# One FFN stage of a Trainium2 encoder block, fed with the un-normalized activations in 512-column matmuls, with the normalization applied to its results

## The chip, the cores and the metric

The kernel runs on one core of one Trainium2 chip. The metric is device time in microseconds (us), the median of several executions; before the change it is 2491.45 us (three runs, 2491.24 to 2491.88). The core has a matrix engine (TensorE, PE in the profile), three engines for elementwise work (VectorE, DVE in the profile; ScalarE, ACT; GpSimd, POOL) and a queue engine (SyncE, SP) that issues most loads. Each takes its own list of instructions, and they wait for one another through semaphores. The numbers of lines (L175 and so on) are those of the kernel before, unless it is said that they belong to the changed kernel.

## What is computed

One encoder layer over 512 tokens of 2048 features, in float32. The change lies in the last third, the SwiGLU feed-forward part:

```python
        u = rms_norm(h, ffn_pre_g[l])
        gate, up = jnp.split(u @ w_gate_up[l], 2, axis=-1)
        f = (jax.nn.silu(gate) * up) @ w_down[l]
        h = h + rms_norm(f, ffn_post_g[l])
```

`rms_norm(h, g)` is h times g (by feature) divided by the root of the mean square of h (by token). D_FF is 5632, so `gate` and `up` have 44 blocks of 128 features each; block j of both together is called pair j here. Activations are kept transposed: 16 tiles of 128 features by 512 tokens.

## The kernel before

**Precision.** A float32 matrix product is made of three matmuls on a rounded format (fp32r): an operand is split into a rounded copy ("hi", a cast on ScalarE) and a remainder ("lo", source minus copy, a subtraction on VectorE), and hi x lo, hi x hi and lo x hi are added up in PSUM. Weights come in chunks of 128 x 1024 (`wchunk`: one load on the SP queue into one of five `raw` buffers, one cast `whi`, one remainder `wlo`; `whi` and `wlo` have three buffers each). Activations are split in 512 columns (`split`), or 256 token columns at a time into one tile whose left half is the copy and whose right half the remainder (`merged`, L166 to L171).

**The feed-forward stages.** The residual stream h2 lies in the 16 tiles `f[i]`. Its split copies `u[i]`, scaled by ffn_pre_g but not by the 1/rms per token, are made on the way (`h2`, L886). Pairs 0, 1 (`interleaved`, tiles f0_0 to f0_3 in PSUM) and pair 2 (`gemm`, f0_4 and f0_5) are multiplied from `u` in 512 columns. The 1/rms, which becomes known after the last h2 tile, is made by `rstd` (four small matmuls r_s, a scale, a power on GpSimd) and spread over the partitions by `by_column` (matmuls r_b, then a copy on ScalarE into the tile `r3`, L922). For these three pairs r3 is applied to the results (L927, L928), since it commutes with the product. silu is on ScalarE (L929), the product of both halves on GpSimd (L930), and the store `a_d` on ScalarE's queue (L931).

**The stage f1** computes pairs 4 and 5 of the title, which the code numbers 3 and 4, counted from zero. It loops over eight weight chunks c (from `w_g0[1]`, rows 2c and 2c + 1 of the reduction). For each i = 2c + k it multiplies `f[i]` by ffn_pre_g and r3 in place (L943), splits it with `merged` into two half-token blocks (b1 for i under 8, b2 from 8 on), and multiplies these in 256 columns (`plain`, L175 to L177: 384 matmuls in all). For i from 8 on it also makes the differences of the Winograd form of Strassen's scheme (`winograd_t`, L219 to L222: four subtractions) and splits them (t12, t34). b11, b2, t12 and t34 are the operands of all later pairs, 5 to 43 (`strassen`, L287 to L336), each of which takes 7 products of quarters.

**What sets the order.** The kernel is recorded in program order, and a scheduler then orders each engine's list by priorities and by its estimate of times, and hands out buffers; an instruction marked with `keep_in_program_order` stays in its place among the marked ones of its engine. In this stage of the kernel before almost nothing is marked. On the chip each list runs in order.

Of the kernel before, what the change touches and what calls it, by code (L numbers as in the profile page):

```python
# [74 lines left out]
def hybrid_block(ctx: ExitStack, tc, xT, vecs, rpb, mask, w_c0, w_qk, w_v, w_gg, w_cg, w_ao, w_co, w_out, w_g0, w_gu, w_dn, outT):  # L75
# [60 lines left out]
    def wchunk(src, name, parts=1, cast=nc.scalar.copy, raw=None, load=nc.sync.dma_start):  # L136
# [5 lines left out]
        for n in range(parts):  # L142
            s = slice(n * w // parts, (n + 1) * w // parts)
            if not loaded:
                load(raw[:, s], src[:, s])
            cast(hi[:, s], raw[:, s])  # L146
            nc.vector.tensor_tensor(out=lo[:, s], in0=raw[:, s], in1=hi[:, s].bitcast(F32), op=ALU.subtract)  # L147
# [18 lines left out]
    def merged(src, name):  # L166

        t = slot(name, F32R)
        nc.scalar.copy(t[:, A], src)  # L169
        nc.vector.tensor_tensor(out=t[:, B], in0=src, in1=t[:, A].bitcast(F32), op=ALU.subtract)  # L170
# [2 lines left out]
    def plain(o, hi, lo, t, first, last):

        nc.tensor.matmul(o, hi, t[:, B], start=first, stop=False, skip_group_check=True)  # L175
        nc.tensor.matmul(o, hi, t[:, A], start=False, stop=False, skip_group_check=True)  # L176
        nc.tensor.matmul(o, lo, t[:, A], start=False, stop=last, skip_group_check=True)  # L177

    def gemm(outs, acts, name, n=None, more=None, cols=slice(0, NT), between=(), pin=False, raw=None, load=nc.sync.dma_start):
# [36 lines left out]

    def winograd_t(u1, u2, t12, t34):

        nc.vector.tensor_tensor(out=t12[:, A], in0=u1[:, B], in1=u1[:, A], op=ALU.subtract)  # L219
# [700 lines left out]
    gemm(  # L920
        [(pf[4 + n], w_gu[n * FT + 2]) for n in range(2)], u, "f0",
        between=(lambda: nc.scalar.copy(r3, by_column(r, "r3", pin=True)),),  # L922
    )
    for j in range(3):
        t = stp.tile([P, 2, NT], F32, tag="S", name=f"sg{j}")
        t, up = t[:, 0], t[:, 1]
        nc.vector.tensor_tensor(out=t, in0=pf[2 * j], in1=r3, op=ALU.mult)  # L927
        nc.vector.tensor_tensor(out=up, in0=pf[2 * j + 1], in1=r3, op=ALU.mult)  # L928
        nc.scalar.activation(t, t, AF.Silu)  # L929
        nc.gpsimd.tensor_tensor(out=t, in0=t, in1=up, op=ALU.mult)  # L930
        nc.scalar.dma_start(a_d[j], t)  # L931
# [3 lines left out]
    b11, b2, b_t12, b_t34 = [], [], [], []  # L935
    pf = [bank(f"f1_{n}") for n in range(4)]
    for c in range(HT):
        hi, lo = wchunk(w_g0[1, c], f"f1_{c}")
        if c == HT - 1:
            first = begun(w_gu[5], "f5")  # L940
        for k in range(2):
            i = 2 * c + k
            nc.vector.scalar_tensor_tensor(out=f[i], in0=f[i], scalar=col(C_FPRE, i), in1=r3, op0=ALU.mult, op1=ALU.mult)  # L943
# [414 lines left out]
```

## Time and profile before

| what | us |
|---|---|
| median of three runs | 2491.45 |
| span of the profiled execution (first to last instruction) | 2489.2 |
| the median less that span: start and end, which the span leaves out | 2.25 |
| PE busy in the span | 2464.8 (99%) |
| DVE busy | 2073.3 (83%) |
| ACT busy | 1246.1 (50%) |
| POOL busy | 493.3 (20%) |
| stage f1 on PE, first matmul to the first of pair 5 | 1211.02 to 1257.09 |

The page gives no time of its own for the profiled execution other than the span. A busy share says that an engine had an instruction in flight; matmuls overlap, so the time that one costs is read from the distance of two starts, not from its duration. A bracket at a row's end tells how long the engine had been idle and what ended the wait.

### The profile page before, as it was taken

Reading aid. Unit: us, or ns where it says so; the run is one execution under the profiler, and the core shown is the slowest. Engines: PE = TensorE matmul, PEld = TensorE weight load, DVE = VectorE, ACT = ScalarE, POOL = GpSimd, SP = SyncE. Lnnn points to the kernel's source line nnn. Section 1 sums busy time; section 2 is a strip of 40 time slices with the busy share of each in tenths; the row PEclk is TensorE's granted clock in tenths of the full one; section 3 lists DMA queues with packets and bytes.
Section 4 is the critical chain, followed back from the end, with each engine's and each line's share of the span. In section 5 each row is a group of like instructions: output and inputs, shape, how many; then the busy total and the mean of one; then the engine's idle time right before and its main releaser. Section 6 shows DMA issues by size and latency. Waiting matters only on the chain. (4 is left out here: it accounts for less than half of the span.)

```text
span 2489.2 us, 36170 instructions
## 1 busy us (share of the span) xinstructions
PE 2464.8 (99%) x13495; PEld 2141.7 (86%) x13495; DVE 2073.3 (83%) x2743; ACT 1246.1 (50%) x1939; POOL 493.3 (20%) x583
## 2 busy tenths in 40 slices
PE   9999999999999999999999999999999999999997
PEld 8888888888888888889998888888888888888887
DVE  5999887497777668878898888889898889989887
ACT  5223333355555434556455555555555565456553
POOL 0110242220000000021111111122222203632352
PEclk9999999999999999999999999999999999999998
DMA  6246222376667544669456655666666678888986
GB/s 215 89 144 207 101 103 101 135 253 196 190 187 228 184 142 136 205 215 301 138 166 178 185 170 171 184 195 213 205 200 195 220 234 238 237 230 255 226 222 195
DMA packets 165104, 472.37 MB, mean 190 GB/s; under 512 B 18752, under 2 KB 30656, under 8 KB 164928
## 3 DMA queue, kind: packets, MB, share of 16 engines
q1 hardware_dynamic: 109584, 334.02, 39.1%
q0 software_dynamic: 32928, 97.54, 18.4%
q10 hardware_dynamic: 22416, 38.50, 4.1%
q8 instruction: 106, 1.74, 0.3%
q14 instruction: 70, 0.57, 0.1%
HBM read 396.06 MB, written 71.30 MB: 188 GB/s over the span
## 5 line engine op out<-in xcount | busy, mean ns | idle before, releaser
L450 DVE SCALAR_TENSOR_TENSOR cv<-z,vec,cv 128x497 f32<-128x497 f32 (+14 forms) x240 | 188.4, 786 | 4.8
L971 POOL TENSOR_TENSOR row<-row,asq 128x512 f32<-128x512 f32 x30 | 54.6, 1821 | 402.8 <-ACT asq L970 402.8
L1126 POOL TENSOR_TENSOR ys<-ys,row 128x512 f32<-128x512 f32 x32 | 57.6, 1801 | 119.8 <-DVE ys L347 100.1
L146 ACT CAST whi_qk<-raw_qk 128x1024 fp32r<-128x1024 f32 x32 | 33.7, 1053 | 79.2 <-PE qk L196 58.2
L147 DVE TENSOR_TENSOR wlo_qk<-raw_qk,whi_qk 128x1024 fp32r<-128x1024 f32 x32 | 40.4, 1262 | 37.9 <-ACT whi_qk L146 37.8
L993 POOL TENSOR_TENSOR an<-an,row 128x512 f32<-128x512 f32 x32 | 55.3, 1729 | 72.1 <-DMA an<-a_d 45.7
L146 ACT CAST whi_y<-raw_y 128x1024 fp32r<-128x1024 f32 x31 | 32.6, 1051 | 64.9 <-PE py L196 52.7
L760 DVE TENSOR_TENSOR gg<-py,gg 128x512 f32<-128x512 f32 x32 | 21.9, 687 | 46.4 <-PE py L197 43.4
L531 POOL TENSOR_TENSOR bm<-braw,msk 128x64 f32<-128x64 f32 x96 | 54.3, 600 | 14.8 <-DMA braw<-in_rpb 14.7
L193 PE MATMUL py<-ycl,whi_y 128*128 128x512 f32 x128 | 49.9, 390 | 0.0
L196 PE MATMUL py<-ych,whi_y 128*128 128x512 f32 x128 | 49.8, 389 | 0.0
L197 PE MATMUL py<-ych,wlo_y 128*128 128x512 f32 x128 | 49.8, 389 | 0.0
L147 DVE TENSOR_TENSOR wlo_y<-raw_y,whi_y 128x1024 fp32r<-128x1024 f32 x31 | 37.8, 1224 | 9.0 <-ACT whi_y L146 8.6
L458 POOL TENSOR_TENSOR csum<-csum,cv 128x512 f32<-128x512 f32 x7 | 12.7, 1816 | 141.4 <-DVE cv L450 141.4
L177 PE MATMUL f<-b,wlo_f 128*128 128x256 f32 x128 | 36.3, 283 | 0.0
L176 PE MATMUL f<-b,whi_f 128*128 128x256 f32 x128 | 36.3, 283 | 0.0
L175 PE MATMUL f<-b,whi_f 128*128 128x256 f32 x128 | 36.3, 283 | 0.0
L146 ACT CAST whi_ca<-raw_ca 128x1024 fp32r<-128x1024 f32 x12 | 12.6, 1054 | 46.3 <-PE cb L196 18.1
L787 POOL DMA_DIRECT2D m_d<-m x8 | 4.4, 555 | 136.9 <-ACT m L169 75.0
L568 ACT ACTIVATE sc<-sc,st 128x256 f32<-128x256 f32 x32 | 16.1, 504 | 30.8 <-DVE st L567 30.8
L1127 POOL DMA_DIRECT2D y_d<-ys x32 | 29.4, 918 | 9.4 <-POOL ys L1126 7.8
L1056 DVE TENSOR_TENSOR sg<-sg,su 128x512 f32<-128x512 f32 x39 | 30.0, 770 | 0.0
(3251 smaller groups left out, 8755.6 us busy)
## 6 DMA issues: line engine op xcount, KB each, us to landing
raw_qk<-in_w_qk SPq DMA_DIRECT2D x32, 512.0 KB, 3.3
raw_w<-in_w_dn SPq DMA_DIRECT2D x24, 512.0 KB, 5.4
a_d<-sg ACTq DMA_DIRECT2D x44, 256.0 KB, 4.0
raw_v<-in_w_v SPq DMA_DIRECT2D x16, 512.0 KB, 4.3
gg<-g_d SPq DMA_DIRECT2D x32, 256.0 KB, 4.1
raw_y<-in_w_co SPq DMA_DIRECT2D x16, 512.0 KB, 3.6
raw_f<-in_w_g SPq DMA_DIRECT2D x16, 512.0 KB, 3.9
an<-a_d POOLq DMA_DIRECT2D x32, 256.0 KB, 5.5
```

What stands on the lines that cost most here:

```text
L146: cast(hi[:, s], raw[:, s])
L147: nc.vector.tensor_tensor(out=lo[:, s], in0=raw[:, s], in1=hi[:, s].bitcast(F32), op=ALU.subtract)
L175: nc.tensor.matmul(o, hi, t[:, B], start=first, stop=False, skip_group_check=True)
L176: nc.tensor.matmul(o, hi, t[:, A], start=False, stop=False, skip_group_check=True)
L193: mmul = nc.tensor.matmul(ps, hi[:, s], al, start=first, stop=False)
L196: nc.tensor.matmul(ps, hi[:, s], ah, start=False, stop=False)
L197: nc.tensor.matmul(ps, lo[:, s], ah, start=False, stop=last)
L450: nc.vector.scalar_tensor_tensor(out=a[:, to], in0=z[:, fr], scalar=col(C_WDW, i * CW + w), in1=a[:, to], op0=ALU.mult, op1=ALU.add)
L531: nc.gpsimd.tensor_tensor(out=bm[:, o + i - i0], in0=raw[:, :, min(max(i, 0), 3) * EC : (min(max(i, 0), 3) + 1) * EC], in1=msk[:, o + i - ...
L971: nc.gpsimd.tensor_tensor(out=row[n], in0=row[n], in1=sq, op=ALU.add)
L993: ins = nc.gpsimd.dma_start(t, a_d[DN_P + k]), nc.gpsimd.tensor_tensor(out=t, in0=t, in1=row[k // KT], op=ALU.mult)
L1126: tc.keep_in_program_order(nc.gpsimd.tensor_tensor(out=t, in0=t, in1=row[n], op=ALU.mult))
```

## The change

Stage f1 takes the split `u[i]` as moving operand, in 512 columns, as pairs 0 to 2 do: 192 matmuls in the place of 384, all products with whi first and then those with wlo. A chunk of its weights now holds rows c and c + 8 (another layout of `w_g0[1]`, made on the host before the launch, as the old one was). r3 is multiplied into its results when they are read from PSUM (`scaled_read`). The operands of the later pairs are made beside it: `blocks(c)` scales f[c] and f[c + 8] and splits b11 and b2, and `differences(c)` makes the four differences in place in f and splits them; the eight splits of the right halves of b1, which only `plain` had read, are gone. VectorE's part of all this, the casts on ScalarE and the casts and remainders of f1's weights are marked to stay in program order: group by group, with the weights of chunk c behind the group of the same number (from chunk 6 on one chunk earlier). r3 is spread in the middle of pair 2's first chunk (after three of its eight row blocks, `EARLY_AT`) and not behind that chunk; group 0 is made while pair 2 is multiplied.

```diff
+                    if early and (c, i, k) == (0, 0, EARLY_AT):
+                        early()
...
+    def blocks(c):
+
+        u1, u2 = f[c], f[c + HT]
+        for i, t in ((c, u1), (c + HT, u2)):
+            tc.keep_in_program_order(
+                nc.vector.scalar_tensor_tensor(
+                    out=t, in0=t, scalar=col(C_FPRE, i), in1=r3, op0=ALU.mult, op1=ALU.mult
+                )
+            )
+        b11.append(merged(u1[:, A], f"b11{c}", pin=True))
+        b2.append([merged(u2[:, cols], f"b2{c}_{n}", pin=True) for n, cols in enumerate((A, B))])
+
+    def differences(c):
+
+        u1, u2 = f[c], f[c + HT]
+        difference(u1[:, A], u1[:, B], u1[:, A])
+        difference(u1[:, B], u2[:, B], u1[:, B])
+        t1 = merged(u1[:, A], f"t12{c}_0", pin=True)
+        difference(u2[:, B], u2[:, B], u1[:, A])
+        t3 = merged(u1[:, B], f"t34{c}_0", pin=True)
+        difference(u2[:, A], u2[:, A], u2[:, B])
+        b_t12.append([t1, merged(u2[:, B], f"t12{c}_1", pin=True)])
+        b_t34.append([t3, merged(u2[:, A], f"t34{c}_1", pin=True)])
+
+    def scaled_read(j, ps, up_ps, t, up):
+
+        for out, src in ((t, ps), (up, up_ps)):
+            tc.keep_in_program_order(nc.vector.tensor_tensor(out=out, in0=src, in1=r3, op=ALU.mult))
+        nc.scalar.activation(t, t, AF.Silu)
+        (nc.gpsimd if j < 3 else nc.vector).tensor_tensor(out=t, in0=t, in1=up, op=ALU.mult)
+
+    def first_gated(j):
+
+        t = stp.tile([P, 2, NT], F32, tag="S", name=f"sg{j}")
+        scaled_read(j, pf[2 * j], pf[2 * j + 1], t[:, 0], t[:, 1])
+        nc.scalar.dma_start(a_d[j], t[:, 0])
+
     gemm(
         [(pf[4 + n], w_gu[n * FT + 2]) for n in range(2)], u, "f0",
-        between=(lambda: nc.scalar.copy(r3, by_column(r, "r3", pin=True)),),
+        early=lambda: nc.scalar.copy(r3, by_column(r, "r3", pin=True)),
+        between=(lambda: blocks(0), lambda: differences(0)),
     )
...
+    def next_weights():
+
+        c = len(weights_of)
+        weights_of.append(wchunk(w_g0[1, c], f"f1_{c}", pin=True))
+
+    def multiply(c):
+
+        hi, lo = weights_of[c]
+        for last in range(2):
+            for k, (ah, al) in enumerate((u[c], u[c + HT])):
+                for n, ps in enumerate(pg):
+                    s = slice((k * 4 + n) * P, (k * 4 + n + 1) * P)
+                    if last:
+                        nc.tensor.matmul(ps, lo[:, s], ah, start=False, stop=c + k == HT, skip_group_check=True)
+                        continue
+                    nc.tensor.matmul(ps, hi[:, s], al, start=c + k == 0, stop=False, skip_group_check=True)
+                    nc.tensor.matmul(ps, hi[:, s], ah, start=False, stop=False, skip_group_check=True)
+
+    for j in range(2):
+        first_gated(j)
+    next_weights()
     for c in range(HT):
-        hi, lo = wchunk(w_g0[1, c], f"f1_{c}")
-        if c == HT - 1:
+        if c + 1 < HT:
+            blocks(c + 1)
+            differences(c + 1)
+        else:
             first = begun(w_gu[5], "f5")
...
+        if c == 1:
+            first_gated(2)
+        while len(weights_of) < min(c + (2 if c < 4 else 3), HT):
+            next_weights()
+        multiply(c)
...
-        nc.scalar.activation(t, pf[2 * j], AF.Silu)
-        nc.vector.tensor_tensor(out=t, in0=pf[2 * j + 1], in1=t, op=ALU.mult)
+        scaled_read(3 + j, pg[2 * j], pg[2 * j + 1], t, slot(f"su{3 + j}"))
```

The lists of PE, POOL and SP outside this stage are the same as before but for two neighbouring loads of the pairs 6 and 7 on SP, which change places; the lists of ACT and DVE differ from the end of pair 2's weights to the first part of pair 6. Three places show how the lists now stand. First PE, where f1 opens; f1_0 to f1_3 are its four PSUM tiles, before:

```order
L175 MATMUL f1_0_10959<-b10_0_10970,whi_f1_0_10964 128x256
L176 MATMUL f1_0_10959<-b10_0_10970,whi_f1_0_10964 128x256
L177 MATMUL f1_0_10959<-b10_0_10970,wlo_f1_0_10965 128x256
L175 MATMUL f1_0_10959<-b10_1_10973,whi_f1_0_10964 128x256
L176 MATMUL f1_0_10959<-b10_1_10973,whi_f1_0_10964 128x256
L177 MATMUL f1_0_10959<-b10_1_10973,wlo_f1_0_10965 128x256
```

and now:

```order
L987 MATMUL f1_0_10968<-u2_0l_10347,whi_f1_0_10985 128x512
L988 MATMUL f1_0_10968<-u2_0h_10346,whi_f1_0_10985 128x512
L987 MATMUL f1_1_10969<-u2_0l_10347,whi_f1_0_10985 128x512
L988 MATMUL f1_1_10969<-u2_0h_10346,whi_f1_0_10985 128x512
L987 MATMUL f1_2_10970<-u2_0l_10347,whi_f1_0_10985 128x512
L988 MATMUL f1_2_10970<-u2_0h_10346,whi_f1_0_10985 128x512
```

A matmul covers all 512 tokens, and needs the weights and the old `u` alone, no block that is made in this stage.

Second ScalarE (ACT), around the cast of f1's weight chunk 2 (whi_f1_2) and the gating of pair 2 (sg2: silu at the ACTIVATE, store to a_d at the DMA). Before:

```order
L929 ACTIVATE sg2_10953<-sg2_10953 128x512
L169 CAST b15_0_11137<-f5_10015 128x256
L169 CAST b15_1_11140<-f5_10015 128x256
L169 CAST b16_0_11174<-f6_10019 128x256
L169 CAST b16_1_11177<-f6_10019 128x256
L169 CAST b17_0_11205<-f7_10023 128x256
L146 CAST whi_f1_2_11100<-raw_f1_2_11099 128x1024
L169 CAST b17_1_11208<-f7_10023 128x256
L931 DMA a_d_10341<-sg2_10953 128x512
```

and now:

```order
L175 CAST t122_1_11068<-f10_10035 128x256
L175 CAST t342_1_11071<-f10_10035 128x256
L952 ACTIVATE sg2_11074<-sg2_11074 128x512
L959 DMA a_d_10341<-sg2_11074 128x512
L148 CAST whi_f1_2_11081<-raw_f1_2_11080 128x1024
L175 CAST b113_11112<-f3_10007 128x256
```

The cast of chunk 2 stood ahead of the store of sg2; it now stands behind it, and behind all casts of group 2.

Third VectorE (DVE), around the remainder of chunk 5 (wlo_f1_5); f5s2 is a sum of weights of pair 5 (its place in the code is L282 of `strassen`). Before:

```order
L147 TENSOR_TENSOR wlo_f1_5_11341<-raw_f1_5_11339,whi_f1_5_11340 128x1024
...
L147 TENSOR_TENSOR wlo_f1_7_11549<-raw_f1_7_11547,whi_f1_7_11548 128x1024
...
L170 TENSOR_TENSOR t3415_0_11651<-t34_15_11640,t3415_0_11651 128x256
L282 TENSOR_TENSOR f5s2_11719<-f5s1_11670,f5q_11553 128x1024
L170 TENSOR_TENSOR t3415_1_11654<-t34_15_11640,t3415_1_11654 128x256
```

and now:

```order
L149 TENSOR_TENSOR wlo_f1_4_11196<-raw_f1_4_11194,whi_f1_4_11195 128x1024
L929 SCALAR_TENSOR_TENSOR f5_10015<-f5_10015,vec_75,r3_10801 128x512
L929 SCALAR_TENSOR_TENSOR f13_10169<-f13_10169,vec_75,r3_10801 128x512
L176 TENSOR_TENSOR b115_11226<-f5_10015,b115_11226 128x256
L280 TENSOR_TENSOR f5s2_11493<-f5s1_11444,f5q_11395 128x1024
L176 TENSOR_TENSOR b25_0_11229<-f13_10169,b25_0_11229 128x256
...
L176 TENSOR_TENSOR t345_1_11248<-f13_10169,t345_1_11248 128x256
L149 TENSOR_TENSOR wlo_f1_5_11253<-raw_f1_5_11251,whi_f1_5_11252 128x1024
L149 TENSOR_TENSOR wlo_f1_6_11259<-raw_f1_6_11257,whi_f1_6_11258 128x1024
```

f5s2, which came behind the last of f1's weights, now stands inside group 5, ahead of the remainders of chunks 5, 6 and 7.

More of the change, by code (lines that the diff above doesn't have):

```diff
@@ L134, in wraw, with wchunk @@
         return wp.tile([P, 1024], F32, tag="raw", name=f"raw_{name}", bufs=5)
-    def wchunk(src, name, parts=1, cast=nc.scalar.copy, raw=None, load=nc.sync.dma_start):
+    def wchunk(src, name, parts=1, cast=nc.scalar.copy, raw=None, load=nc.sync.dma_start, pin=False):
         w = src.shape[-1]
@@ L145, in wchunk @@
                 load(raw[:, s], src[:, s])
-            cast(hi[:, s], raw[:, s])
-            nc.vector.tensor_tensor(out=lo[:, s], in0=raw[:, s], in1=hi[:, s].bitcast(F32), op=ALU.subtract)
+            ins = (
+                cast(hi[:, s], raw[:, s]),
+                nc.vector.tensor_tensor(out=lo[:, s], in0=raw[:, s], in1=hi[:, s].bitcast(F32), op=ALU.subtract),
+            )
+            for i in ins if pin else ():
+                tc.keep_in_program_order(i)
         taps(rate)
@@ L164, in split, with merged, gemm @@
         return hi, lo
-    def merged(src, name):
+    def merged(src, name, pin=False):
         t = slot(name, F32R)
-        nc.scalar.copy(t[:, A], src)
-        nc.vector.tensor_tensor(out=t[:, B], in0=src, in1=t[:, A].bitcast(F32), op=ALU.subtract)
-        return t
[L173 to L179, printed above, removed]
+        ins = (
+            nc.scalar.copy(t[:, A], src),
+            nc.vector.tensor_tensor(out=t[:, B], in0=src, in1=t[:, A].bitcast(F32), op=ALU.subtract),
+        )
+        for i in ins if pin else ():
+            tc.keep_in_program_order(i)
+        return t
+    def gemm(outs, acts, name, n=None, more=None, cols=slice(0, NT), between=(), pin=False, raw=None, load=nc.sync.dma_start, early=None):
         n = n or len(acts)
@@ L920, in hybrid_block @@
     gemm(
         [(pf[4 + n], w_gu[n * FT + 2]) for n in range(2)], u, "f0",
-        between=(lambda: nc.scalar.copy(r3, by_column(r, "r3", pin=True)),),
-    )
[L924 to L931, printed above, removed]
@@ L935, in hybrid_block @@
-    b11, b2, b_t12, b_t34 = [], [], [], []
-    pf = [bank(f"f1_{n}") for n in range(4)]
+        early=lambda: nc.scalar.copy(r3, by_column(r, "r3", pin=True)),
+        between=(lambda: blocks(0), lambda: differences(0)),
+    )
+    pg = [bank(f"f1_{n}") for n in range(4)]
+    weights_of = []
+    def next_weights():
[12 more added lines that the diff above has]
+                    nc.tensor.matmul(ps, hi[:, s], ah, start=False, stop=False, skip_group_check=True)
@@ L1311, in _layout @@
     wi = w_in[0]
-    gu = w_gate_up[0].reshape(KT // 2, 2, P, 2, FT, P)[:, :, :, :, (0, 1, 3, 4)].reshape(KT // 2, 2, P, 2, 2, 2, P)
-    gu = gu.transpose(4, 0, 2, 1, 5, 3, 6).reshape(2, KT // 2, P, 8 * P)
+    gu = w_gate_up[0].reshape(KT, P, 2, FT, P)
+    gu = [
+        gu[:, :, :, n : n + 2].reshape(*by, P, 2, 2, P).transpose(*order, 2, 1 - order[0], 4, 3, 5).reshape(KT // 2, P, 8 * P)
+        for n, by, order in ((0, (KT // 2, 2), (0,)), (3, (2, KT // 2), (1,)))
+    ]
     cw = wi[:, 3 * CONV : 5 * CONV].reshape(KT // 2, 2, P, 2, CT, P)[:, :, :, :, :2]
```

31 lines of the change are left out of this document (7 added, 24 removed).

## The prediction

> **What bounds the kernel now.** I read the page's busy shares first, then a table of stretches around stage f1, then the list of who waited for whom, then the engines' instructions in order of time. The share says PE, and the stretches (busy us in each; the number of instructions in brackets, then granted clock, DMA share and GB/s) say PE in f1 too, with VectorE full beside it:
>
> ```profile
> PE 2464.8 (99%) x13495; PEld 2141.7 (86%) x13495; DVE 2073.3 (83%) x2743; ACT 1246.1 (50%) x1939; POOL 493.3 (20%) x583
> 1195.00:1211.00 16.00, 16.00 (x72) 13.24 (x71) 15.85 (x27) 8.22 (x18) 2.59 (x2) 1.00 0.32 110
> 1211.00:1257.00 46.00, 46.00 (x385) 45.98 (x384) 46.00 (x104) 26.54 (x62) 4.50 (x3) 1.00 0.43 129
> 1257.00:1277.00 20.00, 19.84 (x115) 17.33 (x114) 17.83 (x21) 11.03 (x16) 0.85 (x1) 1.00 0.68 190
> PE f L298 <- ACT f5v L287: 0.2, 1, 0.2
> ```
>
> Clock 1.00, PE without a gap from 1195 to 1257, and one PE wait of 0.2 us behind it: f1 takes as long as its matmuls. VectorE does 46.00 of 46 us without PE ever waiting for it, so it is just fast enough. What a matmul costs is the distance of two starts:
>
> ```profile
> 1205.58 0.39 PE L193 MATMUL f<-u_8l,whi_f 128*128 128x512 f32 x1
> 1211.02 0.28 PE L175 MATMUL f<-b,whi_f 128*128 128x256 f32 x1
> 1257.09 2.00 PE L298 MATMUL f<-b,f5h 128*128 128x512 f32 x8
> ```
>
> 24 matmuls of 512 columns lie between the first two rows: 5.44 us, 0.2267 each. 384 of 256 columns lie between the second and the third: 46.07 us, 0.1200 each.
>
> **What PE gains.** 192 x 0.2267 = 43.53 us in the place of 46.07: 2.54 us less, if nothing makes PE wait. The 512-column row is one of pair 2, with the same `u` as f1 will have.
>
> [...]
>
> **r3 comes sooner.** The spreading moves ahead by 15 of pair 2's matmuls:
>
> ```profile
> 1188.19 0.49 PE L193 MATMUL f<-u_0l,whi_f 128*128 128x512 f32 x1
> 1193.77 1.05 PE L374 MATMUL r_b<-ident,r_r 128*128 128x128 f32 x8
> 1194.86 0.59 ACT L922 COPY r<-r_b 128x512 f32<-128x512 f32 x1
> 1188.61 1.03 POOL L367 TENSOR_TENSOR r_r<-r_v,mhalf 128x4 f32<-128x4 f32 x1 [8.54 <-DVE r_v L365]
> ```
>
> Nine matmuls from 1188.19 on (the first 0.32 by its next start, the others 0.227) end at 1190.3; GpSimd's power is ready at 1189.64, so PE does not wait, and the r_b matmuls are as many as before. From their start to r3's last byte it took 1194.86 + 0.59 - 1193.77 = 1.68 us: r3 stands at 1192.0 in the place of 1195.45. Cost nil, gain 3.4 us of head start for VectorE and ScalarE.
>
> **What f1's weights now stand behind.** PE needs no block, but each chunk needs its cast (whi) and remainder (wlo), and these now stand behind the group of blocks of their number on both engines. Prices, as distances of starts:
>
> ```profile
> 1231.28 0.74 DVE L943 SCALAR_TENSOR_TENSOR f<-f,vec,r 128x512 f32<-128x512 f32 x1
> 1231.94 1.22 DVE L147 TENSOR_TENSOR wlo_f<-raw_f,whi_f 128x1024 fp32r<-128x1024 f32 x1
> 1233.07 0.42 DVE L170 TENSOR_TENSOR b<-f,b 128x256 fp32r<-128x256 f32 x1
> 1233.41 0.42 DVE L219 TENSOR_TENSOR t<-f 128x256 f32<-128x256 f32 x1
> 1217.95 0.41 DVE L219 TENSOR_TENSOR t<-f 128x256 f32<-128x256 f32 x1
> 1218.40 0.41 ACT L169 CAST t<-t 128x256 fp32r<-128x256 f32 x1 [0.95 <-DVE t L219]
> 1230.36 0.40 ACT L169 CAST b<-f 128x256 fp32r<-128x256 f32 x1
> 1230.67 1.04 ACT L146 CAST whi_f<-raw_f 128x1024 fp32r<-128x1024 f32 x1
> ```
>
> A scaling 0.66, a weights' remainder 1.13, a 256-column subtraction 0.34; on ScalarE a block's cast takes 0.40 (the next one starts after 0.31), a weights' cast 1.04; from one engine's end to the other's start 0.04. A group is two scalings (1.32), three remainders, four differences and four remainders (11 x 0.34 = 3.74): 5.06, with its weights 6.19 us on VectorE, against PE's 24 x 0.2267 = 5.44 per chunk. To this come the hand-overs, since the list is fixed and has nothing else to do meanwhile. The second scaling ends 1.40 after the group's start, b2's cast ends at 1.84, and VectorE, free at 1.66, goes on at 1.88: 0.22. Two differences read what the one just before them wrote and wait for its end, 0.11 each. The last block's cast starts when the fourth difference ends, which costs 0.22, and the weights' cast is behind it on ScalarE: 0.31 later it starts, 1.04 later it ends, and VectorE has stood idle for 0.61 more. In all 1.27: a group takes **7.46 us**, 2.02 more than PE's chunk. The lead must pay for that.
>
> **The lead.** Up to the first read of sg0 VectorE has 5.06 + 1.13 (pair 2's last weights) less the one remainder behind it: 1192.0 + 5.85 = 1197.9. What follows stood in the same order before:
>
> ```profile
> 1195.96 0.69 DVE L927 TENSOR_TENSOR sg<-f,r 128x512 f32<-128x512 f32 x1
> 1196.57 0.68 DVE L928 TENSOR_TENSOR sg<-f,r 128x512 f32<-128x512 f32 x1
> 1197.39 1.30 POOL L930 TENSOR_TENSOR sg<-sg 128x512 f32<-128x512 f32 x1 [7.75 <-ACT sg L929]
> 1198.72 0.33 ACTq L931 DMA_DIRECT2D a_d<-sg  x1
> 1199.10 0.63 ACT L929 ACTIVATE sg<-sg 128x512 f32<-128x512 f32 x1 [1.78 <-POOL sg L930]
> 1199.81 1.29 POOL L930 TENSOR_TENSOR sg<-sg 128x512 f32<-128x512 f32 x1 [1.11 <-ACT sg L929]
> 1201.58 1.06 ACT L146 CAST whi_f<-raw_f 128x1024 fp32r<-128x1024 f32 x1 [1.25 <-POOL sg L930]
> 1202.96 1.21 DVE L147 TENSOR_TENSOR wlo_f<-raw_f,whi_f 128x1024 fp32r<-128x1024 f32 x1
> 1213.42 2.73 POOL L930 TENSOR_TENSOR sg<-sg 128x512 f32<-128x512 f32 x1 [12.32 <-ACT whi_f L146]
> ```
>
> ScalarE's list stands still at the store of sg until GpSimd has multiplied (idle 1.78 and 1.25), and the cast of chunk 0 is behind it: 7.0 us from the first read to wlo. So chunk 0 is ready at 1204.9, 6.1 before PE opens f1 at 1211.0, and VectorE is free at 1206.0. Chunk 1: 1206.0 + 7.46 - 1.13 = 1212.4, needed at 1211.0 + 5.44 = 1216.5: no wait.
>
> Chunk 2 stands behind group 2 **and** sg2's store. Group 2 starts at 1213.5 and reaches the first read after 5.06 + 0.44 + 0.22 = 5.7, at 1219.2; the second read ends at 1220.5; GpSimd starts 0.1 later and takes 1.30: 1221.9; from its end to the end of the cast it was 1202.64 - 1201.10 = 1.54: 1223.4. Needed at 1221.9: **PE waits 1.5**. 1.30 and not 2.73, since VectorE has nothing to do during it; at 2.73 (row 1213.42, where it scaled) it would be 1.4 more.
>
> [...]
>
> Chunks 3 and 4: 7.46 against 5.44, **2.0 each**, at 1230.9 and 1238.4.
>
> **The sum inside group 5.** VectorE meets f5s2 there, for which both halves of pair 5's sums must have landed, the second by a load that GpSimd issues and that adds:
>
> ```profile
> 1221.53 0.33 SPq L254 DMA_DIRECT2D f5q<-in_w_gu  x1
> 1221.96 0.37 SPq L99 DMA_DIRECT2D f5s<-in_w_gu  x1
> 1227.58 0.91 POOL L248 DMA_DIRECT2D f5s<-in_w_gu  x1 [11.44 <-DMA f5s<-in_w_gu]
> f5s<-in_w_gu SPq DMA_DIRECT2D x1, 512.0 KB, 5.3
> f5s<-in_w_gu POOLq DMA_DIRECT2D x1, 512.0 KB, 7.6
> f6s<-in_w_gu POOLq DMA_DIRECT2D x1, 512.0 KB, 5.7
> ```
>
> SP's list holds f5s behind the load f5q, which takes the raw buffer that wlo of chunk 3 frees (five buffers: chunks 3 to 7 are in them). That wlo ends at 1230.9 + 1.2 = 1232.1; f5s is issued 0.4 later, lands 5.3 later (1237.8), GpSimd issues 0.3 later, and 5.7 to 7.6 later it is there: 1243.8 to 1245.7. VectorE arrives at 1238.4 + 1.13 + 1.32 + 0.34 = 1241.2 and waits 2.6 to 4.5; I take the middle, less 0.2 for a hand-over that falls into it: 3.4. With f5s2 itself (1.13) chunk 5 comes 7.46 + 1.13 + 3.4 = 12.0 after chunk 4: **PE waits 6.5**. Chunk 6 is next on both lists. Chunk 7 comes two remainders, a group, its hand-overs and one more sum after chunk 5, 2.26 + 5.06 + 1.27 + 1.13 = 9.7, against 10.9: no wait.
>
> **Behind f1** four reads (0.60 each) are new on VectorE in a stretch where it has 2.2 of 20 us free and PE waited 0.2: between 0 and 2.4 us; I take 0.3, since the free time covers nearly all. The eight splits that are gone (8 x 0.34) are in the group's count already. The products that follow read the same operands in the same order: nothing.
>
> **Sum:** -2.5 + 1.5 + 2.0 + 2.0 + 6.5 + 0.3 = **+9.8**. The span of 2489.2 becomes 2499.0; the runs' median lies 2.25 above the span: **2501.2**. Bounds: with hand-overs at nothing but the weights' cast (0.61), the groups take 6.8 and the sum is about +6; with GpSimd at 2.73, the adding load at 7.6 and 2.4 behind f1 it is +14.3. The likeliest case's own range is thus 2497.5 to 2505.7.
>
> **Rivals.** *All hidden.* VectorE's bare work from r3 to chunk 5 is 9.7 (to wlo of chunk 0, with four reads) + 5 x 6.19 + 1.2 + 1.13 = 43.0: 1235.0, against PE's need at 1238.2. Without hand-overs and waits everything fits, and the time is 2491.45 - 2.5 = 2488.9. For it: in the kernel before VectorE was full and PE never waited. Against: there its list mixed other groups' work into the gaps, and rows 1199.10 and 1201.58 show the stand-still. *The adding load is in time* (f5s2 waits for nothing): the sum is 3.4 less, 2497.8. Against: even 5.7 is 2.6 too late. [...] *The change does not do what it says* is excluded for the matmuls, which stand as 192 on PE's list.
>
> **Chances.** Forecast 0.60; load in time or hand-overs cheaper, 2494 to 2498, 0.20; hidden 0.13; the page's gap 0.03; dearer than the bounds 0.04. A measurement of this kernel tells some 0.2% (5 us) from no change: slower than 2496.4 takes the forecast, the two dear cases and two thirds of the second, 0.81; within it 0.16, the hidden case and the rest of the second; faster 0.03, for which the hidden case would need 2.4 us from elsewhere. Range for 8 in 10: 2494 to 2505.5.
>
> **What would show it.** PE's waits should name the casts whi of chunks 2 to 5 (1.5, 2.0, 2.0, 6.5); VectorE should stand before f5s2 for a DMA, and before each wlo for 0.6; ScalarE before the cast of chunk 2 for GpSimd. PE's first matmul of pair 5 should lie some 55 us behind f1's first, not 43.5. If PE shows no wait in f1, the hand-overs are mispriced and the prediction is wrong; if only chunk 5's is missing, the load's time is.

## The result and the profile after

The changed kernel takes **2502.06 us** (median of five runs, 2501.69 to 2506.19) against 2491.24 us (2490.43 to 2491.88) in five runs of the kernel before. The ratio is 1.0045, with a 95% interval of 1.0035 to 1.0056: it is slower by 10.8 us. The span of its profiled execution is 2500.0 us (2489.2 before).

Who waited for whom, on PE between 1180 and 1310 us of the changed kernel (us in total, times, longest):

```profile
PE f L987 <- ACT whi_f L148: 7.9, 4, 2.5
PE r_s L355 <- DVE h_sq L382: 0.2, 1, 0.2
```

There are four waits for casts of f1's weights where the kernel before had none. The stretches ahead of f1, with f1 and behind it (busy us and number of instructions of PE, PEld, DVE, ACT, POOL, then granted clock, DMA share, GB/s) say the same, and that VectorE was not the busier for it:

```profile
1195.00:1211.00 16.00, 16.00 (x73) 13.23 (x72) 11.61 (x25) 6.81 (x14) 2.58 (x2) 1.00 0.30 100
1211.00:1263.00 52.00, 44.05 (x183) 34.93 (x182) 42.76 (x85) 24.94 (x50) 3.06 (x3) 0.97 0.40 115
1263.00:1283.00 20.00, 19.87 (x110) 17.05 (x109) 20.00 (x32) 11.35 (x17) 0.85 (x1) 1.00 0.57 154
```

VectorE worked 42.76 of 52 us, where it had worked 46.00 of 46. The 9.2 us between are idle time inside a list that was waited for. The third number to notice is the granted clock, 0.97 in f1; that was not expected, and it has a section of its own below.

The first matmuls of the chunks 0 to 5 and 7 and of pair 5 on PE, in order of time (start, duration):

```profile
1211.85 0.39 PE L987 MATMUL f<-u_0l,whi_f 128*128 128x512 f32 x1
1217.29 0.39 PE L987 MATMUL f<-u_1l,whi_f 128*128 128x512 f32 x1
...
1224.61 0.50 PE L987 MATMUL f<-u_2l,whi_f 128*128 128x512 f32 x1 [1.72 <-ACT whi_f L148]
1232.22 0.50 PE L987 MATMUL f<-u_3l,whi_f 128*128 128x512 f32 x1 [1.84 <-ACT whi_f L148]
1239.83 0.50 PE L987 MATMUL f<-u_4l,whi_f 128*128 128x512 f32 x1 [1.85 <-ACT whi_f L148]
1249.74 0.50 PE L987 MATMUL f<-u_5l,whi_f 128*128 128x512 f32 x1 [2.54 <-ACT whi_f L148]
...
1260.76 0.39 PE L987 MATMUL f<-u_7l,whi_f 128*128 128x512 f32 x1
1266.20 1.07 PE L296 MATMUL f<-b,f5h 128*128 128x512 f32 x4
```

Where PE does not wait a chunk lasts 5.44 us (1211.85 to 1217.29, 1260.76 to 1266.20), which is 24 x 0.2267: the gain of 2.54 us over eight chunks is there. Over 5.44 us, the distances from the start of chunk 1 to that of chunk 2 and so on are longer by 1.88, 2.17, 2.17, 4.47 and 0.14 us. In all f1 takes 54.35 us in the place of 46.07: **8.28 us of the 10.8**. The other 2.5 lie ahead of f1, which opens 0.83 later, and behind pair 6's first product (1.7). Of the 0.83, 0.36 lie in pair 2, where the early spreading of r3 found GpSimd's power not ready. The other 2.2 are not shown to come from the change: the table of the experiments tells how much these two places differ from one program to the next.

VectorE's own list shows where the time went (the bracket is the idle time ahead of the instruction and what ended it); rows of the remainders of chunks 0, 2, 3 and 5, of two splits and of the sum f5s2:

```profile
1205.87 1.23 DVE L149 TENSOR_TENSOR wlo_f<-raw_f,whi_f 128x1024 fp32r<-128x1024 f32 x1 [4.20 <-ACT whi_f L148]
...
1224.59 1.23 DVE L149 TENSOR_TENSOR wlo_f<-raw_f,whi_f 128x1024 fp32r<-128x1024 f32 x1 [3.05 <-ACT whi_f L148]
...
1227.67 0.76 DVE L176 TENSOR_TENSOR b<-f,b 128x256 fp32r<-128x256 f32 x2 [0.19 <-ACT b L175]
...
1231.26 0.43 DVE L176 TENSOR_TENSOR t<-f,t 128x256 fp32r<-128x256 f32 x1 [0.19 <-ACT t L175]
1232.20 1.22 DVE L149 TENSOR_TENSOR wlo_f<-raw_f,whi_f 128x1024 fp32r<-128x1024 f32 x1 [0.52 <-ACT whi_f L148]
...
1244.06 1.23 DVE L280 TENSOR_TENSOR f5s<-f5s,f5q 128x1024 f32<-128x1024 f32 x1 [1.36 <-DMA f5s<-in_w_gu]
...
1249.72 2.36 DVE L149 TENSOR_TENSOR wlo_f<-raw_f,whi_f 128x1024 fp32r<-128x1024 f32 x2 [0.52 <-ACT whi_f L148]
```

The casts that ended the two long waits stood behind the stores of sg on ScalarE, and those behind GpSimd's product; the sum waited for GpSimd's adding load. ScalarE, GpSimd and SP:

```profile
1192.29 0.59 ACT L963 COPY r<-r_b 128x512 f32<-128x512 f32 x1 [3.64 <-PE r_b L372]
...
1204.78 1.05 ACT L148 CAST whi_f<-raw_f 128x1024 fp32r<-128x1024 f32 x1 [1.84 <-POOL sg L953]
...
1223.52 1.04 ACT L148 CAST whi_f<-raw_f 128x1024 fp32r<-128x1024 f32 x1 [1.90 <-POOL sg L953]
...
1189.09 1.95 POOL L365 TENSOR_TENSOR r_r<-r_v,mhalf 128x4 f32<-128x4 f32 x1 [9.13 <-DVE r_v L363]
...
1221.77 1.29 POOL L953 TENSOR_TENSOR sg<-sg 128x512 f32<-128x512 f32 x1 [17.47 <-ACT sg L952]
1238.57 0.91 POOL L246 DMA_DIRECT2D f5s<-in_w_gu  x1 [15.51 <-DMA f5s<-in_w_gu]
...
1233.89 0.37 SPq L100 DMA_DIRECT2D f5s<-in_w_gu  x1
```

### The profile page after: what moved, and what is told of

It is laid out like the page before. It is cut to its first block, busy times and chain, and to the rows that moved or that the text cites. A ratio compares the mean times of both kernels' runs of the same rounds, so it can differ in the third digit from the quotient of the medians.

```text
span 2500.0 us, 35791 instructions
## 1 busy us (share of the span) xinstructions
PE 2465.6 (99%) x13303; PEld 2131.1 (85%) x13303; DVE 2073.2 (83%) x2739; ACT 1246.5 (50%) x1931; POOL 489.6 (20%) x583
## 5 line engine op out<-in xcount | busy, mean ns | idle before, releaser
L149 DVE TENSOR_TENSOR wlo_f<-raw_f,whi_f 128x1024 fp32r<-128x1024 f32 x20 | 24.4, 1223 | 9.9 <-ACT whi_f L148 9.9
L148 ACT CAST whi_v<-raw_v 128x1024 fp32r<-128x1024 f32 x16 | 16.8, 1050 | 24.2 <-PE pv L517 17.5
L201 PEld LDWEIGHTS py<-ych,whi_y 128*128 128x128 f32 x128 | 24.0, 188 | 5.0
```

Of the source, the lines that this page charges most:

```text
L148: cast(hi[:, s], raw[:, s]),
L201: nc.tensor.matmul(ps, hi[:, s], ah, start=False, stop=False)
```

## The experiments

Two theories stood against each other. **Idle:** VectorE's marked list is one chain from r3 to chunk 5, its idle time arrives at PE, and without it the shorter stage is to be had. **Work:** a group with its weights is 6.19 us of VectorE against 5.44 of PE, so the shorter stage can't be fed in any order. The table has all runs (us). "f1" is the distance from its first matmul to the first of pair 5; "chunk 5 late" is the start of chunk 5 less that of f1, less the 27.20 that five chunks of 5.44 take; "pair 5" goes to the first product with a t operand of pair 6, "rest" from there to the end of the span; the last column has the stretches in which the granted clock was 0.50.

| kernel | median | f1 opens | chunk 5 late | f1 | pair 5 | rest | clock 0.50 |
|---|---|---|---|---|---|---|---|
| before | 2491.2 | 1211.0 | - | 46.07 | 22.7 | 1209.4 | none |
| changed | 2502.06 | 1211.9 | 10.69 | 54.35 | 22.7 | 1211.1 | 3.4 us |
| marks off | 2489.56 | 1211.6 | 0.00 | 43.52 | 22.6 | 1209.3 | none |
| stores on GpSimd | 2497.75 | 1210.7 | 6.95 | 53.34 | 22.7 | 1209.3 | 6.8 |
| sum later | 2500.55 | 1212.2 | 8.38 | 52.08 | 23.6 | 1210.8 | 3.4 |
| sg2 behind | 2500.72 | 1210.6 | 9.20 | 54.47 | 22.7 | 1211.2 | 3.4 and 3.4 |
| weights first | 2499.68 | 1210.3 | 4.61 | 52.84 | 24.0 | 1210.8 | 6.8 |
| marks off, r3 late | 2490.13 | 1211.9 | 0.00 | 43.52 | 23.2 | 1210.1 | none |
| changed, r3 late | 2505.38 | 1211.8 | 13.55 | 58.81 | 22.7 | 1210.5 | 6.8 and 3.4 |
| waits filled | 2499.85 | 1210.6 | 10.66 | 54.33 | 23.1 | 1210.0 | none |
| casts ahead | 2496.47 | 1210.3 | 0.49 | 49.00 | 23.9 | 1211.4 | 3.4 |
| sum loaded early | 2498.67 | 1210.6 | 8.63 | 52.31 | 22.7 | 1210.9 | 3.4 |
| all three | 2493.16 | 1212.2 | 0.39 | 45.49 | 24.6 | 1208.3 | none |
| marks off, stores on GpSimd | 2488.01 | 1210.5 | 0.00 | 43.52 | 22.3 | 1209.4 | none |

The opening of f1 scatters over 1.9 us and the rest over 3.1, in one profiled execution each. The opening does not go with what was edited. The rest is longer (1210.5 to 1211.4) in seven of the eight kernels with a stretch at 0.50 than in the six without (1208.3 to 1210.1), although that stretch lies in f1. In the changed kernel the 1.7 us are small waits of PE far behind the stage (0.43 us in pair 37, 0.59 in the down projection, where it was 0.15 before) and some 0.6 us behind PE's last product; why they differ stays open. So f1 and chunk 5 are read to tenths from the traces, and the medians to about 1 us. The changed kernel was not run again beside the experiments; the kernel before was, and its medians there were 2490.95 to 2491.15.

**1. Marks off.** The marks of order on VectorE's work, on the casts and on f1's weights are removed (the one on the spreading of r3 stays); the instructions stay:

```diff
-        weights_of.append(wchunk(w_g0[1, c], f"f1_{c}", pin=True))
+        weights_of.append(wchunk(w_g0[1, c], f"f1_{c}"))
...
-        tc.keep_in_program_order(nc.vector.tensor_tensor(out=out, in0=x, in1=y, op=ALU.subtract))
+        nc.vector.tensor_tensor(out=out, in0=x, in1=y, op=ALU.subtract)
```

and so in `blocks`, `differences` and `scaled_read`.

> All marks of order in the stage are taken off (the scheduler orders the same instructions). Theory 'idle': the changed kernel loses by VectorE standing idle inside a fixed list (9.2 of 52 us in f1), not by its work. With other work in the gaps PE waits for no weights, f1 takes 43.5 to 44 us from its first matmul to the first of pair 5, and the time is about 2489 (2491.2 - 2.5 + 0.3). Rival 'work': a group with its weights is 6.19 us of VectorE against 5.44 of PE, whatever the order: from the remainder of chunk 0 at 1207.1 on, chunk 7 comes 7 x 6.19 + 1.13 later, 1251.6, and f5s2 with it at 1252.7, against PE's need at 1249.9: waits of 2 to 3 us remain, f1 takes about 46.5, the time is 2491 to 2492. If the hand-overs belong to the split and not to the order, more: 2496 to 2502.

Measured: 2489.56 us, ratio to before 0.9992 (0.9984 to 1.0001), and f1 in 43.52 us without a wait. Its stretch of f1 in the table of stretches:

```profile
1211.00:1255.00 44.00, 44.00 (x196) 36.45 (x195) 41.95 (x91) 23.95 (x53) 4.83 (x3) 1.00 0.47 138
```

and four neighbouring rows of VectorE in order of time:

```profile
1228.51 1.09 DVE L176 TENSOR_TENSOR b<-f,b 128x256 fp32r<-128x256 f32 x3
1229.52 0.41 DVE L922 TENSOR_TENSOR f<-f 128x256 f32<-128x256 f32 x1
1229.85 1.21 DVE L149 TENSOR_TENSOR wlo_f<-raw_f,whi_f 128x1024 fp32r<-128x1024 f32 x1
1230.99 0.41 DVE L922 TENSOR_TENSOR f<-f,f 128x256 f32<-128x256 f32 x1
```

The remainder of chunk 4 stands here between the first and the second difference of its group, with its cast long made, and VectorE goes from one row to the next without idle time. VectorE has the same instructions to do and PE the same matmuls; "work" expected 46.5 us and waits. It falls: the groups are heavier than PE's chunk, but the lead (chunk 0's remainder ends nearly 5 us ahead of f1) is enough when little stands idle, 2.05 us of 44.

**2. The three stores of sg on GpSimd's queue**, behind the product that they store:

```diff
-        nc.scalar.dma_start(a_d[j], t[:, 0])
+        nc.gpsimd.dma_start(a_d[j], t[:, 0])
```

> Only the stores of sg0, sg1 and sg2 go from ScalarE's queue to GpSimd's, behind the product that they store. Theory 'idle': ScalarE no longer stands still for GpSimd ahead of the casts of chunk 0 and chunk 2 (1.84 and 2.11 ahead of the first, 1.90 ahead of the second in the changed kernel), the remainder of chunk 0 comes some 2 to 3 us sooner and that of chunk 2 another 2 sooner, the wait at chunk 2 vanishes and chunk 5 moves by the sum: 2502.1 - 4.7 = 2497.4 (2495.5 to 2499). Rival 'work': nothing is won ahead of chunk 3, since groups at 6.19 and more run behind anyway: 2501 to 2502. Second rival: GpSimd's stores delay the adding load of pair 5 (0.9 us an issue, three of them): no change of chunk 5, 2502.

Measured: 2497.75 us, 4.3 less than the changed kernel; chunk 2 is not waited for, chunk 5 comes 3.7 us sooner. The stall of ScalarE's list at the stores is worth these 3.7 us. In the profiled execution f1 shrank by 1.0 only, though: the granted clock was 0.50 while PE did the matmuls of chunk 5, and no wait followed that could hide it. Of the 4.0 us by which the span is shorter, the other 3.0 lie in f1's opening (1.2) and in the rest (1.8), so that the median came near the expected 2497.4 partly by luck. The stretches with chunk 5 and behind it:

```profile
1244.80:1250.60 5.80, 5.79 (x14) 4.53 (x15) 5.61 (x9) 2.43 (x5) 0.00 (x0) 0.50 0.54 170
1250.60:1264.00 13.40, 13.40 (x60) 11.11 (x59) 10.50 (x21) 7.05 (x14) 0.86 (x1) 1.00 0.69 200
```

**3. f5s2 behind the last remainder of f1**, and **10. its load ahead of f1**, part the two halves of chunk 5's extra time:

```diff
-            nc.vector.tensor_tensor(out=t, in0=a, in1=b, op=op)
+            ins = nc.vector.tensor_tensor(out=t, in0=a, in1=b, op=op)
+            if name == "f5":
+                issued_behind(ins, pinned[1])
```

(`pinned[1]` is the last marked remainder, that of chunk 7.)

> Only f5s2 moves: it is ordered behind the remainder of the last weight chunk of f1 on VectorE. Theory 'idle': 1.13 of work and 1.36 of waiting for the adding load leave group 5; the gap between the first matmuls of chunk 4 and chunk 5 goes from 9.91 to 7.5 us; the second product of pair 5 may wait up to 1 us for the sum: 2502.1 - 2.5 + 0.8 = 2500.4 (2499.3 to 2501). Rival 'it only moves': the wait for the sum comes back in full behind f1: 2502. Rival 'clock': the 9.91 are due to the granted clock of 0.70 in chunk 4's matmuls and not to f5s2: the gap stays above 9.

```diff
+    s1_5 = sums(w_gu[FT + 5], "f5")
     for j in range(2):
         first_gated(j)
...
-            w_gu[j], w_gu[FT + j], op, f"f{j}", j, sums(w_gu[FT + j], f"f{j}", load_in_order) if j < 7 else None,
+            w_gu[j], w_gu[FT + j], op, f"f{j}", j, s1_5 if j == 5 else sums(w_gu[FT + j], f"f{j}", load_in_order) if j < 7 else None,
```

> Only the two loads of pair 5's sum (f5s1) move, ahead of f1; the scheduler then puts f5s2 into group 4, ahead of the last remainder there. Theory 'idle': the wait of 1.36 for the adding load goes, and f5s2's 1.13 covers 0.19 and 0.52 of hand-overs: the gap from chunk 3 to chunk 4 becomes about 8.0 (7.61), that from chunk 4 to chunk 5 about 7.6 (9.91): 2502.1 - 1.36 - 0.7 = 2500.0 (2499.3 to 2500.8). Rival 'the load is hidden anyway' (the granted clock of 0.50 made the gap): 2502.

With the sum later, chunk 5 starts behind chunk 4 by 7.61 us, like the chunks ahead of it (9.91 in the changed kernel, 7.5 expected); pair 5 then takes 0.9 us longer and waits 1.05 us for VectorE (f5v, an addition to one of its products; the row does not name the sum). First the rows of the sum later, chunks 4 and 5 and pair 5's wait:

```profile
1240.17 0.50 PE L992 MATMUL f<-u_4l,whi_f 128*128 128x512 f32 x1 [0.25 <-ACT whi_f L149]
1247.78 0.50 PE L992 MATMUL f<-u_5l,whi_f 128*128 128x512 f32 x1 [1.87 <-ACT whi_f L149]
1279.44 1.63 PE L301 MATMUL f<-t,f5h 128*128 128x512 f32 x6 [1.05 <-DVE f5v L337]
```

and of the sum loaded early, f5s2 and the remainder of chunk 4 on VectorE:

```profile
1237.34 1.22 DVE L280 TENSOR_TENSOR f5s<-f5s,f5q 128x1024 f32<-128x1024 f32 x1
1238.81 1.22 DVE L149 TENSOR_TENSOR wlo_f<-raw_f,whi_f 128x1024 fp32r<-128x1024 f32 x1
```

The sum waits for nothing there, and the hand-over ahead of the remainder, 0.52 elsewhere, lies under it. The gaps from chunk 3 to 4 and 4 to 5 are 7.62 and 7.84 (8.0 and 7.6 expected), and f1 is shorter by 2.04 (2.06 expected). The medians are 1.5 (expected 1.7) and 3.4 us (expected 2.1) below the changed kernel. That the clock made the gap, the rival, is excluded: chunk 5 comes 2.1 to 2.3 us sooner although both runs have their spell.

**4. sg2's gating behind the weights of chunk 2:**

```diff
-        if c == 1:
-            first_gated(2)
         while len(weights_of) < min(c + (2 if c < 4 else 3), HT):
             next_weights()
+        if c == 1:
+            first_gated(2)
```

> Only the gating of pair 2 moves behind the weights of chunk 2. Theory 'idle': VectorE's idle time ahead of the remainder of chunk 2 falls from 3.05 to 0.6, chunk 2 is not waited for (or under 0.3); ScalarE's wait for GpSimd then falls ahead of group 3's first cast and costs some 1.0 to 1.3 there: net 1.0 to 1.6, 2502.1 - 1.4 = 2500.7. Rival 'work': the 1.7 us that PE does not wait at chunk 2 it waits at chunk 3, in full: 2502.

Measured: 2500.72 us. Chunk 2 is not waited for; chunk 3 is, by 2.7 us, yet starts 1.34 us sooner than in the changed kernel (19.03 after f1's opening, 20.37 there), and chunk 5 1.49 sooner. So part of the stall is only moved, and the rest of it is won, as "idle" had it. The rows of the chunks 3 and 5:

```profile
1229.62 0.50 PE L987 MATMUL f<-u_3l,whi_f 128*128 128x512 f32 x1 [2.55 <-ACT whi_f L148]
1246.99 0.50 PE L987 MATMUL f<-u_5l,whi_f 128*128 128x512 f32 x1 [4.03 <-ACT whi_f L148]
```

In its profiled execution two spells of low clock took that back within f1 (54.47), and f1 opened 1.3 us sooner; that the median is just what was expected (2500.7) is therefore partly luck.

**5. The weights of chunk c + 1 ahead of their group:**

```diff
     for c in range(HT):
+        while len(weights_of) < min(c + 2, HT):
+            next_weights()
         if c + 1 < HT:
             blocks(c + 1)
...
-        while len(weights_of) < min(c + (2 if c < 4 else 3), HT):
-            next_weights()
```

> Only the place of f1's weights in the marked order changes: chunk c + 1 ahead of the group of that number instead of behind it. Theory 'idle': VectorE's list is as long as before and holds the same idle time, so the waits move to the later chunks and hardly shrink: chunks 2 to 4 come in time, chunks 5 to 7 wait (about 4, 2 and 2 us), and pair 5 starts about 1 to 1.5 us sooner than in the changed kernel but waits for its blocks or sums by as much: 2501.8 (2500 to 2502.5). Rival 'weights behind blocks': it is the place of the weights that costs the time, since PE needs no block in f1. Then no chunk is waited for, f1 takes 43.5 to 45 us, and the time is 2489 to 2492.

Measured: 2499.68 us, 0.3 outside the range that was expected and far from the rival's. This had looked like the natural cure, since PE needs no block in f1. The waits move instead:

```profile
1226.59 0.39 PE L987 MATMUL f<-u_3l,whi_f 128*128 128x512 f32 x1
1242.08 0.79 PE L987 MATMUL f<-u_5l,whi_f 128*128 128x512 f32 x1 [4.04 <-ACT whi_f L148]
1257.53 0.50 PE L987 MATMUL f<-u_7l,whi_f 128*128 128x512 f32 x1 [1.83 <-ACT whi_f L148]
1278.63 1.62 PE L296 MATMUL f<-t,f5h 128*128 128x512 f32 x6 [1.37 <-DVE f5v L332]
```

to chunks 5 and 7 and into pair 5. A list with the same idle time in it is late somewhere else.

**6 and 7. r3 spread where it was before**, in the unmarked and in the changed kernel:

```diff
-        early=lambda: nc.scalar.copy(r3, by_column(r, "r3", pin=True)),
-        between=(lambda: blocks(0), lambda: differences(0)),
+        between=(lambda: (nc.scalar.copy(r3, by_column(r, "r3", pin=True)), blocks(0)), lambda: differences(0)),
```

> The unmarked kernel of the first experiment with r3 spread where it was before, behind pair 2's first chunk; r3 stands some 3 us later. Theory 'idle': the unmarked list has that slack (remainder of chunk 0 there 5 us ahead of PE's need, that of chunk 7 3.7 us ahead of its first matmul and more ahead of its own use), so PE waits for nothing or under 0.5: 2489.6, as without it. Rival 'head start': the early r3 is what pays for the shorter stage: PE waits 2 to 3 us in f1, 2491.5 to 2492.5.

> The changed kernel with r3 spread where it was before. Theory 'idle': VectorE's fixed list is a chain from r3 to chunk 5, so what r3 loses arrives at PE, less what the waits for GpSimd and for the adding load absorb: the wait at chunk 2 grows by 1.4 to 3.1 us, 2503.5 to 2505 (I take 2504). Rival 'head start is slack': 2502.

Measured: 2490.13 us without the marks (ratio to before 0.9996, 0.9988 to 1.0005; f1 in 43.52, no wait) and 2505.38 with them. Copy of r3 in the changed kernel with the late spread, and its chunk 2:

```profile
1195.62 0.59 ACT L963 COPY r<-r_b 128x512 f32<-128x512 f32 x1
1227.43 0.80 PE L986 MATMUL f<-u_2l,whi_f 128*128 128x512 f32 x1 [4.61 <-ACT whi_f L148]
```

r3 is 3.3 us later than in the changed kernel (1195.62 against 1192.29), and chunk 5 starts 2.8 us later (1252.53 against 1249.74): the marked list passes most of its late start on. The median is 3.3 higher, 0.4 above the expected range, but f1 is 4.5 us longer, since two spells of low clock fall into it. The unmarked one has the slack, and does not need the early spread for f1.

**8. PE's waits filled** with 40 matmuls that nothing reads, 7, 8, 8 and 17 ahead of chunks 2 to 5:

```diff
+FILL = (0, 0, 7, 8, 8, 17, 0, 0)
...
+    keep = abank("keep")
...
+        for _ in range(FILL[c]):
+            nc.tensor.matmul(keep, u[0][0][:, :P], u[0][0], start=True, stop=True, skip_group_check=True)
```

> The changed kernel with 40 matmuls more that nothing reads, into a free PSUM tile, put into PE's waits ahead of chunks 2 to 5 (7, 8, 8 and 17 of them, 1.59, 1.81, 1.81 and 3.85 us at 0.2267 each, against waits of 1.88, 2.17, 2.17 and 4.47). Theory 'stops slow the clock': the spells of about 3.5 us at a granted clock of 0.50 seen in f1 in the changed kernel and in three experiments, and in none that has no wait, come of PE's stops. Filled, the clock stays at 1.00, the five runs lie within 2 us (4.5 in the changed kernel), the median is 2501 to 2502.5, since the waits themselves stay. Rival 'chance': the clock falls in this stage whether PE stops or not; a spell is seen and the scatter stays. Rival 'filler is on the path': the matmuls delay the chunks: 2503 and more.

Measured: 2499.85 us (2498.79 to 2502.38). The whole of f1 in the table of stretches:

```profile
1210.60:1265.00 54.40, 53.90 (x234) 43.28 (x233) 45.22 (x90) 25.36 (x51) 3.07 (x3) 1.00 0.43 128
```

and the fillers and the first matmul of chunk 5 on PE:

```profile
1244.27 4.01 PE L982 MATMUL keep<-u_0h 128*128 128x512 f32 x17
1248.49 0.50 PE L991 MATMUL f<-u_5l,whi_f 128*128 128x512 f32 x1 [0.21 <-ACT whi_f L149]
```

The clock stayed at 1.00 and f1 took 54.33 us, as in the changed kernel (54.35): the waits are VectorE's, not the clock's. The scatter of the five runs is 3.6 us (4.5 in the changed kernel, under 2 expected), so that part is not confirmed. The median lies 2.2 below the changed kernel's, and below the expected range; of the 1.9 us by which the span is shorter, 1.2 lie in f1's opening and 1.1 behind pair 6's first product (pair 5 takes 0.4 more), so the fillers are not shown to have won anything.

**9. ScalarE's cast of a chunk ahead of the casts of its group**, VectorE's marked list as it was:

```diff
         if c + 1 < HT:
+            if len(casts) < HT:
+                next_cast()
             blocks(c + 1)
```

(`next_cast` loads and casts the next chunk; `next_weights` makes its remainder alone.)

> Only ScalarE's order changes: the cast of f1's chunk c + 1 stands ahead of that group's block casts instead of behind them; VectorE's marked list stays as it was (its unmarked sum f5s2 shifts by three rows). Theory 'idle': the 0.52 us ahead of four remainders and the 3.05 ahead of that of chunk 2 go, less 1.0 to 1.3 that ScalarE's stop at sg2's store gives back in group 3; and PE, which needs only the cast for the first 16 matmuls of a chunk (3.63 us), waits for remainders instead. Remainder of chunk 5: 1249.7 - 2.1 - 2.5 + 1.2 = 1246.3 against 1242.7: 3 to 4 us of waits in f1 instead of 10.8, so 46.5 to 47.5; pair 5 then waits for its blocks, up to 2 us: 2502.1 - 7.3 + 2 = 2496.8 (2495 to 2499). Rival 'ScalarE is full': a cast of 1.04 ahead of the blocks delays each group by as much as it saves: 2501 to 2502.

Measured: 2496.47 us, ratio to before 1.0020 (1.0011 to 1.0029). Chunk 5 is late by 0.49 in the place of 10.69, and what PE waits for is now the remainder, in the middle of a chunk:

```profile
1238.02 0.39 PE L1005 MATMUL f<-u_5l,whi_f 128*128 128x512 f32 x1
1244.91 2.08 PE L1003 MATMUL f<-u_5h,wlo_f 128*128 128x512 f32 x4 [3.09 <-DVE wlo_f L991]
```

The waits are 3.3 us as expected; f1 ends 1.5 above the expected range, since a spell of low clock followed, and pair 5 takes 1.3 longer, not 2.

**11. Three edits together** (casts ahead, stores on GpSimd, sum loaded early), still marked:

> The marked order with three edits at once: casts ahead (as in the experiment of that name), the three sg stores on GpSimd's queue, pair 5's sum loaded ahead of f1. Theory 'idle': the terms add, PE waits for nothing or under 1 us in f1 (43.5 to 44.5 us), the granted clock stays at 1.00, and pair 5 waits some 2 us for blocks and sums, which VectorE now reaches behind the weights: 2502.1 - 10.8 + 2 = 2493.3 (2492 to 2495). Rival 'work': VectorE at 6.19 a group against 5.44 keeps 2 to 3 us of waits in f1: 2495.5 to 2497.

Measured: 2493.16 us, ratio to before 1.0008 (0.9999 to 1.0016). One wait is left in f1, and the clock is 1.00:

```profile
1244.81 1.19 PE L1003 MATMUL f<-u_5h,wlo_f 128*128 128x512 f32 x4 [1.27 <-DVE wlo_f L991]
```

f1 takes 45.49 us, 1 us more than expected, and pair 5 the 2 us more that were. Under the marks f1 is 8.9 us shorter than in the changed kernel; against f1 without a wait (43.52) 2.0 are left there, and 1.9 stand in pair 5, which finds its blocks later. So the stage won back 6.9 us. The median is 8.9 lower because the rest was 2.8 us shorter in this program, which no edit here is shown to cause: that it came out at the expected 2493.3 is partly luck.

**12. Marks off and the stores on GpSimd:**

> The unmarked kernel with the three sg stores on GpSimd's queue as well. Theory 'idle': PE has no wait left in f1 in the unmarked kernel, so nothing is to be won: 2489.5 (2488.8 to 2490.3), f1 in 43.5. Rival 'reads behind f1': ScalarE's and VectorE's slack still decides behind f1, and the freer ScalarE gives 0.5 us or more: 2488 to 2489.

Measured: 2488.01 us (2486.45 to 2490.76), ratio to before 0.9988 (0.9979 to 0.9997): the lowest median of all, 2.9 us below the kernel before, with an interval that ends just short of 1, and 14.1 below the changed kernel. It lies below the expected range and in the rival's. f1 takes 43.52 us as with the marks off alone, so nothing was won there. Of the 1.3 us by which the span is shorter than with the marks off alone, 1.07 lie in f1's opening and 0.3 in pair 5. The gain is thus not shown to come from the stores, and the rival is not excluded. GpSimd's product of sg0 is far slower here, and nobody waits for it:

```profile
1195.64 4.16 POOL L951 TENSOR_TENSOR sg<-sg 128x512 f32<-128x512 f32 x1 [6.53 <-DVE sg L949]
```

## Why the prediction was right, and where it was not

Forecast 2501.2, measured 2502.06, in the range and with the sign. By its steps:

- **What PE gains**, 2.54 us: 5.44 a chunk, right. A smaller gain, the first of the two dear cases in the chances (0.03), is shown by no run, and the same rows exclude it.
- **r3** at 1192.0: 1192.88 (1192.29 + 0.59). Pair 2 opened 0.47 later, and GpSimd's power took 1.95 us and not 1.03, so that the matmuls of the spreading started at 1191.09 and not at 1190.3. The prediction had put this at no cost to PE; pair 2 took 23.19 us in the place of 22.83.
- **The lead:** chunk 0's remainder started at 1205.87, not at 1204.9; 0.9 of the 1.0 came from r3, and the group and the two stalls were priced rightly. Chunk 1 had no wait, as forecast.
- **Chunk 2**, 1.5: 1.88. GpSimd's product took 1.29 beside an idle VectorE, the cheap price.
- **Chunks 3 and 4**, 2.0 each: 2.17 each. A group with its weights takes 7.61 us (7.46 forecast). The experiments put this on the chain: taking single pieces of idle time away moves chunk 5 by them.
- **The sum inside group 5**, 6.5: **4.47; this is the term that was mis-sized.** The mechanism was right. With f5s2 itself and the group that makes 9.91 us from chunk 4 to chunk 5, where 12.0 were forecast. f5s was issued at 1233.89 (1232.5 forecast), but landed sooner (GpSimd issued 4.7 us later, not 5.6), the adding load took at most 5.5 us (1238.57 to 1244.06) where the middle of 5.7 and 7.6 had been taken, and VectorE came at 1242.7 and not 1241.2. So it waited 1.36 us and not 3.4. That is the rival "the adding load is in time" by more than half.
- **Behind f1**, 0.3: nothing; pair 5 takes 22.7 us before and after.
- **The sum:** f1 came to +8.3 where +9.5 was forecast (the parts of the sum without the 0.3). That the total was so near is partly luck: 2.5 us ahead of f1 and behind pair 6 have no step in the prediction, and all but the 0.36 in pair 2 are unexplained. By f1 alone it would have been 2499.7.
- **The signs** that it named were all seen: PE's waits name the casts of chunks 2 to 5, VectorE stands before f5s2 for a DMA and 0.52 us before the remainders, ScalarE before the cast of chunk 2 for GpSimd, and 54.35 us lie between the two openings (some 55 forecast).
- **What it did not see:** the spell of low clock. In the profiled execution it cost f1 nothing, since chunk 4's matmuls, slowed, were done by 1247.2 and the cast of chunk 5 came at 1249.7. In other executions it may fall on matmuls that no wait follows; whether that makes the changed kernel's scatter (4.5 us) stays open, since the kernel before scattered by 5.7 in 20 runs beside the experiments (2489.58 to 2495.24).
- **The hidden case** (2488.9) is what the instructions can do: 2489.56 and 2488.01 without the marks. The prediction's price of the hand-overs decided rightly that they would not do it in this order.

## What to carry to other kernels

A fixed order on an engine that is nearly full has to be priced with its hand-overs, not by its work: 0.1 to 0.5 us here and there made 6.19 us of work into 7.61, and one stall behind another engine's store came on top, where the scheduler's mixture of groups ran the same work with 2.05 us of idle time in 44. A chain that is late stays late: moving the weights ahead, or one stall elsewhere, moved the wait, while idle time that was taken off brought chunk 5 forward by most of it (3.7 us for the stores, 2.3 and 2.1 for the sum). And an issue of a store that waits for a third engine (here ScalarE's for GpSimd, idle for 2.11, 1.84 and 1.90 us) should not stand in the list of an engine that others wait for.
